# An SSM branch fused into a projection pass: paired output products, paired in-chunk kernels, one scan per part, and a higher scheduling level

## The chip, the cores and the metric

The kernel runs on one NeuronCore of a Trainium2 chip. The metric is the device time of one execution in microseconds (us), the median over several runs. The engines are TensorE (PE, with its weight loads PEld), VectorE (DVE), ScalarE (ACT), GpSimd (POOL) and SyncE (SP), which here issues every DMA of the program.

## The reference

One layer of a hybrid encoder over 2048 prompt tokens and 64 sample tokens, D = 1024, all in float32. `x @ w_in` gives q, k, v and u, 512 columns each. q and k go through a partial rotary and into differential attention (8 heads, two softmax maps each, block-causal mask). u goes through a diagonal SSM and a gated linear unit (GLU). Both halves meet in `@ w_out`, then follow a layer norm, a feed-forward block with 4096 hidden columns, and a second layer norm. The part that matters here is the SSM:

```
32 groups of 16 channels, each with 64 complex states:
  h[l] = lb * h[l-1] + (bb_re + i bb_im) u[l]        prompt from 0, sample from the state h0
  y[l] = Re(C h[l]) + d * u[l]
  z    = gelu(y) @ w_glu + b_glu ; out = z[:512] * sigmoid(z[512:])
```

## The kernel before

**Chunks.** The 2048 prompt steps are cut into 256 chunks of T = 8 steps and the sample into 8; with one column kept for the sample's starting state there are NJ = 265 columns. Within a chunk the SSM is a matrix product with a kernel matrix `km`; between chunks it is a scan over the 265 columns.

**Batches.** The 32 groups are worked in four batches of 8 groups, which lie in four pairs: group 2q on partitions 0 to 63, group 2q+1 on 64 to 127 (64 states each). `ssm_build` makes a batch's matrices: `bb`, `em` (input to state), `gf` (state to output), the kernels `psk` (PE products of `bb` and `gf`, 64 states by 16 channels, one group at a time), which go by way of the DRAM tensor `KP` into `km`, and the turning factors `et` (some 40 POOL instructions). `ssm_run` loads `ug`, makes the states' inputs `psi` on PE, copies them from PSUM into `z` (real part by ACT, imaginary part by DVE), turns `z` into `v` with `et` (5 DVE instructions), scans, turns back, and then makes one output product `psy` a group: two matmul instructions of 128 rows with `km`, then four of 64 rows with `gf` and `v`. GELU follows as Square (ACT), a DVE instruction, Tanh (ACT), a DVE instruction, and a DMA into the DRAM tensor `GY`. Every float32 matmul shows as two instructions in the trace.

**Buffers.** `psy` has two PSUM banks (`PSB`), `psi` and `psk` share two (`IB`), `gy` has two buffers (`GB`), `z`, `vt`, `vx`, `em` and `et` one each. `ep` in the building and `vx` in the run share one slot.

**Order.** A planner orders each engine's instructions ahead of time: among those that are ready by its own simulated time it takes the one of highest priority, which is program order unless a `level(n)` raises it. While the pass for q and k (`proj_qk`, 17 tiles of 128 tokens; PE tile `pm`, transposes `pt`, outputs `s_q`, `s_k`) is written out, ten steps of the SSM generator are written after each of its tiles (`R1`), so that all SSM steps stand in program order among the first four tiles. `level(U8)` around them is 0, so nothing is raised. From the seventh tile `cache_keys` adds its own copies. After the pass follows the attention, at a level above all of this (`HIP`), whose output accumulator `oT` needs a PSUM bank that the SSM holds until its end; and GLU (`za`, `zb`, `gyg`, `whg`) as filling, which needs all of `GY`. On PE a full-size product in the pass is three matmuls (`mm3`).

Of the kernel before, what the change touches and what calls it, by code (L numbers as in the profile page):

```python
# [67 lines left out]
WGB = 2  # L68
PARTS = [1, 0, 0, 0]
A0S = 0  # L70
U8 = 0
VVB = 2
VB = 2
U5, U6 = 2, 0
# [39 lines left out]
def build(nc, tc, io, ctx):  # L114
# [25 lines left out]
    def tt(e, out, a, b, op):  # L140
        e.tensor_tensor(out=out, in0=a, in1=b, op=op)  # L141
# [529 lines left out]
    def ssm_disc(kp, sp):  # L671

        NC_ = G // 2
        k.ss = ss = K()
        a = sp.tile([128, 3, NC_], F32, name="adisc")
        dma(out=a, in_=io["adisc"])
        sh = [128, NC_]
        t = lambda nm: (kp if nm in ("fr", "fi", "rho") else sp).tile(sh, F32, name=nm)
        dt, x, mag, ang = t("dt"), t("xx"), t("mag"), t("ang")
        exp_exact(sp, dt, a[:, 2], sh, "dx")  # L680
        tt(dve, x, a[:, 0], dt, ALU.mult)
        exp_exact(sp, mag, x, sh, "dx")
# [24 lines left out]
        tt(dve, fr, fr, t2, ALU.add)  # L707
        tt(dve, fr, fr, den, ALU.mult)
        tt(dve, fi, li, a[:, 0], ALU.mult)
        tt(dve, t2, nr, a[:, 1], ALU.mult)  # L710
        tt(dve, fi, fi, t2, ALU.subtract)
        tt(dve, fi, fi, den, ALU.mult)
        ss.fr, ss.fi = fr, fi

        ss.rho = rho = t("rho")
        tt(dve, rho, mag, mag, ALU.mult)
        tt(dve, rho, rho, rho, ALU.mult)
        tt(dve, rho, rho, rho, ALU.mult)
        ss.u = kp.tile([128, 2, 8, NC_], F32, name="uu")
        q = sp.tile([128, 2, NC_], F32, name="uq")  # L720
        for n in range(10):
            w = ss.u[:, :, n - 2] if n > 1 else sp.tile([128, 2, NC_], F32, name="uv%d" % (n + 1))
            tt(dve, q, v, v, ALU.mult)
            dve.scalar_tensor_tensor(out=w[:, 1], in0=v[:, 0], scalar=2.0, in1=v[:, 1], op0=ALU.mult, op1=ALU.mult)
            tt(dve, w[:, 0], q[:, 0], q[:, 1], ALU.subtract)
            tt(dve, q, w, w, ALU.mult)
            tt(dve, q[:, 0], q[:, 0], q[:, 1], ALU.add)
            dve.tensor_scalar(out=q[:, 0], in0=q[:, 0], scalar1=-0.5, scalar2=1.5, op0=ALU.mult, op1=ALU.add)
            tt(dve, w, w, b2(q[:, 0]), ALU.mult)
            v = w  # L730
        ss.zz = kp.tile([C, 1, 112], F32, name="zz")
        pool.memset(ss.zz, 0.0)
        dma(out=KP[:, :, 0:112], in_=ss.zz.to_broadcast([C, G, 112]))
        ss.dsb = kp.tile([C, G], F32, name="dsb")
        dma(out=ss.dsb, in_=io["dT"])
        ss.fin = kp.tile([128, 2, 2, 16], F32, name="hfin")

# [8 lines left out]
    def ssm_build(w, bt):  # L746

        ss = k.ss  # L750
        HG = SSM_HG
        HP = HG // 2
# [4 lines left out]
        m.km = w.kp.tile([128, HG, 128], F32, tag="km", name="km", bufs=MB)  # L757
        m.em = w.kp.tile([128, HP, 2, 128], F32, tag="em", name="em", bufs=1)
        m.gf = w.kp.tile([128, 2, HP, 9, C], F32, tag="gf", name="gf", bufs=MB)
        m.et = w.kp.tile([128, 2, HP, NJ], F32, tag="et", name="et", bufs=EB)  # L760
        bc = bp.tile([128, 2, 2, HP, C], F32, tag="bc", name="bc")
        dma(out=bc[:, 0], in_=io["bP"][:, :, qs, :])
# [31 lines left out]
            act.activation(out=m.em[:, :, ri, :], in_=pse, func=AF.Copy)  # L794
        powers(m.gf, bc[:, 1], 9, True)
        yield
        k0 = bp.tile([128, HG, 128], F32, tag="btm", name="k0")[0:C]
        dd = bp.tile([C, HG, C], F32, tag="dd", name="dd")
        for e in range(2):
            psk = pm.tile([C, HP, 128], F32, tag="pi", name="psk", bufs=IB)  # L800
            o = slice(e * 64, e * 64 + 64)
            for q in range(HP):
                for ri in range(2):
                    pe.matmul(psk[:, q, :], lhsT=bb[o, ri, q, :], rhs=m.gf[o, ri, q, 0:8, :].rearrange("p t c -> p (t c)"),
                              start=ri == 0, stop=ri == 1)
            act.activation(out=k0.rearrange("c (q e) n -> c e q n", e=2)[:, e], in_=psk, func=AF.Copy)
        tt(dve, dd, ss.dsb[:, gs].unsqueeze(2).to_broadcast([C, HG, C]), ident[0:C, 0:C].unsqueeze(1).to_broadcast([C, HG, C]), ALU.mult)
        tt(dve, k0[:, :, 0:C], k0[:, :, 0:C], dd, ALU.add)
        dma(out=KP[:, gs, 112:240], in_=k0)
        for n in range(T):  # L810
            dma(out=m.km[n * C:(n + 1) * C, :, :], in_=KP[:, gs, n * C:n * C + 128])

# [4 lines left out]
        for l in range(1, 8):  # L817
# [3 lines left out]
            for ri in range(2):  # L821
                tt(pool, e[:, ri, :, n:2 * n], e[:, ri, :, 0:n], ss.u[:, 0, l, qs].unsqueeze(2).to_broadcast([128, HP, n]), ALU.mult)
                tt(pool, tmp[:, ri], e[:, 1 - ri, :, 0:n], us, ALU.mult)
                tt(pool, e[:, ri, :, n:2 * n], e[:, ri, :, n:2 * n], tmp[:, ri], (ALU.subtract, ALU.add)[ri])
        pool.tensor_copy(out=e[:, :, :, JP:NJ], in_=e[:, :, :, 0:NJ - JP])
        w.mats = m
        yield

    def ssm_run(w, m, bt):
# [7 lines left out]
        for s in range(T):  # L837
            dma(out=ug[(7 - s) * C:(8 - s) * C, :, :], in_=US.rearrange("(g c) s j -> s c g j", c=C)[s, :, gs, :])

        z = bp.tile([128, 2, HP, NJ], F32, tag="z", name="z", bufs=ZB)  # L840
        vt = bp.tile([128, 2, HP, NJ + 1], F32, tag="vt", name="vt")
        v = vt[:, :, :, 1:NJ + 1]
        vx = bp.tile([128, HP, NJ], F32, tag="vx", name="vx")
# [3 lines left out]
        for q in range(HP):  # L847
            for ri in range(2):
                psi = pm.tile([128, 512], F32, tag="pi", name="psi", bufs=IB)
                for e in range(2):  # L850
                    o = slice(e * 64, e * 64 + 64)
                    pe.matmul(psi[o, :NJ], lhsT=m.em[:, q, ri, o], rhs=ug[:, 2 * q + e, :], start=True, stop=True)
                if ri == 0:
                    act.activation(out=z[:, ri, q, :], in_=psi[:, :NJ], func=AF.Copy)
                else:
                    dve.tensor_copy(out=z[:, ri, q, :], in_=psi[:, :NJ])
            if q % 2:
                yield
        dve.tensor_copy(out=z[:, :, :, JP], in_=h0)
# [7 lines left out]
        turn(v, z, (ALU.add, ALU.subtract))  # L867
        yield
        for ri in range(2):
            for q in range(HP):  # L870
                for c0, c1, i in ((0, JP, 0.0), (JP + 1, NJ, h0[:, ri, q:q + 1])):
                    dve.tensor_tensor_scan(out=z[:, ri, q, c0:c1], data0=ss.rho[:, bt * HP + q:bt * HP + q + 1].to_broadcast([128, c1 - c0]),
                                           data1=v[:, ri, q, c0:c1], initial=i, op0=ALU.mult, op1=ALU.add)
        turn(v, z, (ALU.subtract, ALU.add))
        for i, j in enumerate((JP - 1, NJ - 1)):
            pool.tensor_copy(out=ss.fin[:, i, :, qs], in_=v[:, :, :, j])
        yield
        for g in range(HG):
            psy = pm.tile([128, 512], F32, tag="ps", name="psy")
            y = psy[:, :NJ]  # L880
            o = slice(g % 2 * 64, g % 2 * 64 + 64)
            pe.matmul(y, lhsT=m.km[:, g, :], rhs=ug[:, g, :], start=True, stop=False)
            for ri in range(2):
                pe.matmul(y, lhsT=m.gf[o, ri, g // 2, 1:9, :].rearrange("p t c -> p (t c)"), rhs=vt[o, ri, g // 2, 0:NJ], start=False, stop=ri == 1)

            gy = sp.tile([128, NJ], F32, tag="gy", name="gy", bufs=GB)
            act.activation(out=gy, in_=y, func=AF.Square, scale=math.sqrt(0.044715))
            dve.scalar_tensor_tensor(out=gy, in0=gy, scalar=1.0, in1=y, op0=ALU.add, op1=ALU.mult)
            act.activation(out=gy, in_=gy, func=AF.Tanh, scale=GC)
            dve.scalar_tensor_tensor(out=gy, in0=gy, scalar=1.0, in1=y, op0=ALU.add, op1=ALU.mult)  # L890
            gg = bt * HG + g
            dma(out=GY[gg * C:(gg + 1) * C, :, :].rearrange("c t j -> t c j"), in_=gy)
            if g % 4 == 3:
                yield

    def ssm_all(c2):
# [562 lines left out]
```

## Time and profile before

| what | value |
|---|---|
| median of 3 runs | 3173.56 us (3170.77 to 3175.68) |
| the profiled execution | 3174.97 us |
| its span, first to last instruction | 3173.1 us |
| PE busy | 2909.3 us (92%) |
| DVE busy | 1761.8 us (56%) |
| ACT busy | 1504.2 us (47%) |
| POOL busy | 1636.2 us (52%) |

Outside the span lie 1.9 us. Busy shares are averages over stages with different limits; the pass for q and k with the SSM fills roughly 209 to 527 us of the span, the start of the attention 527 to 590 us, and after that attention, GLU and the feed-forward blocks share the engines.

### The profile page before, as it was taken

The numbers are of one execution on the slowest core, as the hardware profiler recorded it, in microseconds if no ns is written. First come the engines' busy times: TensorE is split into PE (matmuls) and PEld (weight loads), VectorE is DVE, ScalarE is ACT, GpSimd is POOL, SyncE is SP. The second block draws the span as 40 slices with busy tenths as digits, with TensorE's granted clock in tenths as the row PEclk, the third lists the DMA queues.
The fourth block names the chain that finished last, engine by engine and source line by source line (L and its number), as shares of the span: only waits on it lengthen the run. The fifth ranks groups of instructions, "written<-read, shape, count | busy, mean of one in ns | idle before, by whom it ended". The sixth has DMA issues, their size and how long they took to land.

```text
span 3173.1 us, 46490 instructions
## 1 busy us (share of the span) xinstructions
PE 2909.3 (92%) x15648; PEld 2423.9 (76%) x15648; DVE 1761.8 (56%) x4631; ACT 1504.2 (47%) x2905; POOL 1636.2 (52%) x1552
## 2 busy tenths in 40 slices
PE   8999998998898999998689999986899998899996
PEld 7976666896687888786589888864777776788885
DVE  7126866677867665567876666654222226322225
ACT  3222223776775766665567766522232322332332
POOL 2236761455654666565546666534445544544443
PEclk9999998798899999998789999998899998899998
DMA  6368875658534444446434333265223322422221
GB/s 189 128 194 212 219 204 166 202 155 276 147 107 131 130 134 119 119 118 213 144 114 129 100 110 107 76 230 179 74 83 94 89 83 80 130 80 77 80 84 56
DMA packets 420195, 425.47 MB, mean 134 GB/s; under 512 B 53458, under 2 KB 313042, under 8 KB 418932
## 3 DMA queue, kind: packets, MB, share of 16 engines
q1 hardware_dynamic: 419956, 422.50, 45.0%
q8 instruction: 123, 2.02, 0.3%
q14 instruction: 116, 0.95, 0.1%
HBM read 328.76 MB, written 93.64 MB: 133 GB/s over the span
## 4 chain that ended last, share of the span: by engine, by line
PE 55%; DVE 12%; DMA 11%; POOL 6%; issue 4%; ACT 3%; SPq 1%; POOLq 0%; DVEq 0%; ACTq 0%
PE pd L136 7%; PE pd L137 7%; PE pd L138 7%; PE pu L136 5%; PE pu L138 5%; PE pu L137 5%; DMA raw<-in_w_up 4%; PE oT L575 4%; PE tps L559 3%; PE sps L512 3%; DMA raw<-in_w_down 2%; POOL dl L133 2%; POOL fwl L133 2%; DVE acc L141 2%; DMA raw<-in_ln_g 2%
## 5 line engine op out<-in xcount | busy, mean ns | idle before, releaser
L133 POOL TENSOR_TENSOR dl<-raw,dh 128x512 fp32r<-128x512 f32 x336 | 432.8, 1301 | 294.5 <-ACT dh L130 286.3
L133 POOL TENSOR_TENSOR fwl<-raw,fwh 128x512 fp32r<-128x512 f32 x256 | 332.3, 1300 | 380.2 <-ACT fwh L130 355.3
L136 PE MATMUL pu<-bxh,fwh 128*128 128x256 f32 (+2 forms) x1472 | 496.3, 339 | 26.0 <-ACT fr L1167 17.0
L515 DVE TENSOR_SCALAR_CACHE_REDUCE s<-sps 128x512 f32<-128x512 f32 (+5 forms) x688 | 402.9, 600 | 210.9 <-PE sps L512 132.3
L141 POOL TENSOR_TENSOR s<-s 128x512 f32<-128x512 f32 (+3 forms) x344 | 382.6, 1139 | 237.4 <-ACT s L543 237.0
L138 PE MATMUL pu<-bxh,fwl 128*128 128x256 f32 (+2 forms) x1472 | 491.4, 337 | 7.0 <-POOL fwl L133 6.1
L137 PE MATMUL pu<-bxl,fwh 128*128 128x256 f32 (+2 forms) x1472 | 490.6, 334 | 0.0
L136 PE MATMUL pd<-dh,hh 128*128 128x512 f32 (+1 forms) x1088 | 426.5, 400 | 18.6 <-DVE acc L141 10.1
L137 PE MATMUL pd<-dl,hh 128*128 128x512 f32 (+1 forms) x1088 | 430.8, 396 | 0.7 <-POOL dl L133 0.7
L141 DVE TENSOR_TENSOR acc<-acc,pd 128x512 f32<-128x512 f32 (+1 forms) x384 | 254.3, 682 | 302.1 <-PE pd L138 300.8
L523 ACT ACTIVATE s<-s,nm 128x1024 f32<-128x1024 f32 (+9 forms) x416 | 365.8, 881 | 116.7 <-DVE nm L520 113.0
L138 PE MATMUL pd<-dh,hl 128*128 128x512 f32 (+1 forms) x1088 | 419.5, 396 | 0.0
L130 ACT ACTIVATE dh<-raw 128x512 fp32r<-128x512 f32 x336 | 209.2, 628 | 353.8 <-PE pd L138 209.1
L130 ACT ACTIVATE fwh<-raw 128x512 fp32r<-128x512 f32 x256 | 160.5, 628 | 378.9 <-DMA raw<-in_w_up 243.0
L136 PEld LDWEIGHTS pu<-bxh,fwh 128*128 128x128 f32 x1472 | 283.7, 193 | 68.9 <-ACT fr L1167 28.5
L132 DVE CAST hh<-fr 128x256 fp32r<-128x256 f32 (+2 forms) x184 | 111.2, 604 | 397.3 <-ACT fr L1168 397.0
L138 PEld LDWEIGHTS pu<-bxh,fwl 128*128 128x128 f32 x1472 | 282.2, 193 | 40.7 <-POOL fwl L133 15.3
L137 PEld LDWEIGHTS pu<-bxl,fwh 128*128 128x128 f32 x1472 | 283.8, 193 | 26.4
L575 PE MATMUL oT<-w,vt 128*128 128x256 f32 (+3 forms) x1296 | 258.2, 301 | 18.2 <-DVE w L133 12.8
L136 PEld LDWEIGHTS pd<-dh,hh 128*128 128x128 f32 (+1 forms) x1088 | 202.0, 186 | 63.1 <-DVE acc L141 12.0
L575 PEld LDWEIGHTS oT<-w,vt 128*128 128x128 f32 (+1 forms) x1296 | 211.3, 202 | 48.1 <-DVE w L133 20.4
L512 PE MATMUL sps<-kst,qst 96*128 96x512 f32 (+2 forms) x544 | 218.6, 419 | 20.9 <-DVE s L515 18.5
(273 smaller groups left out, 5890.0 us busy)
## 6 DMA issues: line engine op xcount, KB each, us to landing
raw<-in_w_up SPq DMA_DIRECT2D x256, 256.0 KB
raw<-in_w_down SPq DMA_DIRECT2D x256, 256.0 KB
kst<-s_k SPq DMA_DIRECT2D x64, 384.0 KB
raw<-in_w_out SPq DMA_DIRECT2D x80, 256.0 KB
xr<-in_xT SPq DMA_DIRECT2D x64, 256.0 KB
vt<-s_v SPq DMA_DIRECT2D x32, 512.0 KB
qst<-s_q SPq DMA_DIRECT2D x64, 192.0 KB
raw<-in_ln_g SPq DMA_DIRECT2D x36, 256.0 KB
```

What stands on the lines that cost most here:

```text
L130: act.activation(out=dst_hi, in_=src, func=AF.Copy)
L132: hi_eng.tensor_copy(out=dst_hi, in_=src)
L133: (lo_eng or dve).tensor_tensor(out=dst_lo, in0=src, in1=dst_hi.bitcast(F32), op=ALU.subtract)
L136: pe.matmul(ps, lhsT=lh, rhs=rh, start=start, stop=False)
L137: pe.matmul(ps, lhsT=lh, rhs=rl, start=False, stop=False)
L138: pe.matmul(ps, lhsT=ll, rhs=rh, start=False, stop=stop)
L141: e.tensor_tensor(out=out, in0=a, in1=b, op=op)
L512: pe.matmul(ps[:nr, :e - c0], lhsT=qst[m][0:96, q], rhs=self.keys(m, 96, c0, e), start=True, stop=True)
L515: dve.tensor_scalar(out=s[:nr, o:o + c1 - c0], in0=ps[:nr, :c1 - c0], scalar1=1.0, scalar2=None, op0=ALU.mult, op1=ALU.max, accum_out=self ...
L523: act.activation(out=x, in_=x, func=AF.Exp, bias=nm, accum_out=self.ls[:nr, m, p:p + 1])
L559: pe.transpose(out=ps[:kr, i * nr:i * nr + nr], in_=self.s[t, 0, k_ * 128 // SC][:nr, o:o + kr], identity=ident[:nr, :nr])
L575: pe.matmul(self.oT[:, t * nr:(t + n) * nr], lhsT=vt[k_ // 8][:kr, k_ % 8, :], rhs=w[:kr, e, i * nr:(i + n) * nr], start=(k_ == 0 and e == ...
```

## The change

Five things are changed, all in the SSM. (1) `U8 = 1`: the SSM's steps have a raised level and stand ahead of the pass in the planner's choice. (2) The output products are made for the two groups of a pair in turn: both `km` products, then for the real and the imaginary part one `gf` product of each group; the GELU instructions of the two are interleaved. (3) The kernels within a chunk are made by pairs: `bz` holds `bb` of both groups beside zeros, so that one product of 128 rows and 32 columns replaces two of 64 rows and 16 columns; `dsb`, `id2`, `dd`, `k0` follow that layout, and the write into `KP` becomes two DMAs. (4) One scan of 4 x 266 columns for each of real and imaginary part replaces 16 scans a batch: a factor table `rh`, zero at the first column and at the sample's start, cuts it. (5) The copies of `psi` into `z` all go to ACT.

```diff
-U8 = 0
+U8 = 1
...
-        ss.dsb = kp.tile([C, G], F32, name="dsb")
+        ss.dsb = kp.tile([2 * C, G // 2], F32, name="dsb")
+        ss.id2 = kp.tile([2 * C, C], F32, name="id2")
+        tt(dve, ss.id2, ident[0:2 * C, 0:C], ident[0:2 * C, C:2 * C], ALU.add)
...
+        m.rh = w.kp.tile([128, HP, NJ + 1], F32, tag="rh", name="rh", bufs=EB)
...
+        bz = bp.tile([128, 2, HP, 2, C], F32, tag="bz", name="bz")
+        pool.memset(bz, 0.0)
         for e in range(2):
-            psk = pm.tile([C, HP, 128], F32, tag="pi", name="psk", bufs=IB)
             o = slice(e * 64, e * 64 + 64)
-            for q in range(HP):
-                for ri in range(2):
-                    pe.matmul(psk[:, q, :], lhsT=bb[o, ri, q, :], rhs=m.gf[o, ri, q, 0:8, :]...
-            act.activation(out=k0.rearrange("c (q e) n -> c e q n", e=2)[:, e], in_=psk, func=AF.Copy)
+            pool.tensor_copy(out=bz[o, :, :, e, :], in_=bb[o])
+        psk = pm.tile([2 * C, HP, 128], F32, tag="pi", name="psk", bufs=IB)
+        for q in range(HP):
+            for ri in range(2):
+                pe.matmul(psk[:, q, :], lhsT=bz[:, ri, q]..., rhs=m.gf[:, ri, q, 0:8, :]...
+        act.activation(out=k0, in_=psk, func=AF.Copy)
...
-        dma(out=KP[:, gs, 112:240], in_=k0)
+        for e in range(2):
+            dma(out=KP.rearrange("c (q e) n -> e c q n", e=2)[e, :, qs, 112:240], in_=k0[e * C:e * C + C])
...
+        pool.tensor_copy(out=m.rh, in_=ss.rho[:, qs].unsqueeze(2).to_broadcast([128, HP, NJ + 1]))
+        pool.memset(m.rh[:, :, 0:JP + 2:JP + 1], 0.0)
...
-                if ri == 0:
-                    act.activation(out=z[:, ri, q, :], in_=psi[:, :NJ], func=AF.Copy)
-                else:
-                    dve.tensor_copy(out=z[:, ri, q, :], in_=psi[:, :NJ])
+                act.activation(out=z[:, ri, q, :], in_=psi[:, :NJ], func=AF.Copy)
...
-            for q in range(HP):
-                for c0, c1, i in ((0, JP, 0.0), (JP + 1, NJ, h0[:, ri, q:q + 1])):
-                    dve.tensor_tensor_scan(out=z[:, ri, q, c0:c1], data0=ss.rho[...].to_broadcast([128, c1 - c0]),
-                                           data1=v[:, ri, q, c0:c1], initial=i, op0=ALU.mult, op1=ALU.add)
+            dve.tensor_tensor_scan(out=zt[:, ri]..., data0=m.rh..., data1=vt[:, ri]...,
+                                   initial=0.0, op0=ALU.mult, op1=ALU.add)
...
-        for g in range(HG):
-            (one psy: km product, two gf products, GELU, DMA)
+        for q in range(HP):
+            ys = [pm.tile([128, 512], F32, tag="ps", name="psy")[:, :NJ] for e in range(2)]
+            for e, y in enumerate(ys):
+                pe.matmul(y, lhsT=m.km[:, 2 * q + e, :], rhs=ug[:, 2 * q + e, :], start=True, stop=False)
             for ri in range(2):
+                for e, y in enumerate(ys):
+                    o = slice(e * 64, e * 64 + 64)
+                    pe.matmul(y, lhsT=m.gf[o, ri, q, 1:9, :]..., rhs=vt[o, ri, q, 0:NJ], start=False, stop=ri == 1)
+            (Square and first DVE instruction of both, then Tanh, second DVE instruction and DMA of both)
```

## Rows read from the trace of the kernel before

**Rows 1.** Busy time by stretch (us of each engine, instructions; TensorE clock, DMA share, GB/s).

```profile
209.00:527.00 318.00, 296.02 (x1397) 212.30 (x1398) 225.69 (x347) 90.88 (x189) 191.54 (x295) 0.97 0.77 204
...
527.00:590.00 63.00, 47.88 (x164) 34.87 (x164) 35.46 (x141) 38.30 (x105) 15.44 (x20) 0.55 0.81 251
590.00:720.00 130.00, 129.76 (x1076) 128.70 (x1076) 95.78 (x374) 101.72 (x262) 72.03 (x93) 0.99 0.51 154
```

**Rows 2.** PE in order of time, batch 2 (start us, us, what; idle before).

```profile
392.11 0.72 PE L884 MATMUL psy<-vt,gf 64*128 64x265 f32 x4
392.76 0.67 PE L852 MATMUL psi<-ug,em 128*64 128x265 f32 x4
...
398.55 0.71 PE L882 MATMUL psy<-ug,km 128*128 128x265 f32 x2
399.19 1.16 PE L884 MATMUL psy<-vt,gf 64*128 64x265 f32 x4
400.28 0.71 PE L882 MATMUL psy<-ug,km 128*128 128x265 f32 x2
```

**Rows 3.** PE in order of time, the kernels of batch 2.

```profile
298.23 3.24 PE L804 MATMUL psk<-gf,bb 64*16 64x128 f32 x32 [1.76 <-POOL gf L141]
301.40 0.50 PE L136 MATMUL pm<-wh,xh 128*128 128x512 f32 x1
```

**Rows 4.** Instructions by line (count; busy us, mean ns of one; idle before).

```profile
L872 DVE TENSOR_TENSOR_SCAN z<-rho,vt 128x256 f32<-128x256 f32 x32 | 22.6, 706 | 0.0
L872 DVE TENSOR_TENSOR_SCAN z<-rho,h,vt 128x8 f32<-128x8 f32 x32 | 6.8, 214 | 0.0
L854 ACT ACTIVATE z<-psi 128x265 f32<-128x265 f32 x16 | 6.2, 390 | 33.0 <-DVE vx L141 21.9 <-PE psi L852 11.1
L806 ACT ACTIVATE k<-psk 16x512 f32<-16x512 f32 x8 | 4.6, 578 | 8.8 <-PE psk L804 5.1 <-POOL cvv L133 2.8 <-issue 0.8
L132 POOL CAST ckh<-ckr 128x512 fp32r<-128x512 f32 x8 | 5.3, 668 | 6.8 <-DMA ckr<-in_ckT 6.3 <-issue 0.5
```

**Rows 5.** DVE in order of time: turns of the first and the last batch.

```profile
281.75 3.35 DVE L141 TENSOR_TENSOR vt<-z,et 128x2120 f32<-128x2120 f32 x1 [1.85 <-POOL et L141]
305.68 1.25 DVE L141 TENSOR_TENSOR vt<-vt,vx 128x1060 f32<-128x1060 f32 x1
492.99 2.37 DVE L141 TENSOR_TENSOR vt<-z,et 128x2120 f32<-128x2120 f32 x1 [0.87 <-PE psy L884]
500.58 1.25 DVE L141 TENSOR_TENSOR vt<-vt,vx 128x1060 f32<-128x1060 f32 x1
516.16 1.26 DVE L141 TENSOR_TENSOR vt<-vt,vx 128x1060 f32<-128x1060 f32 x1
```

**Rows 6.** ACT in order of time: batch 1's building, and a copy into z.

```profile
245.97 0.63 ACT L130 ACTIVATE xh<-xr 128x512 fp32r<-128x512 f32 x1 [9.28 <-DMA xr<-in_xT]
247.98 1.08 ACT L794 ACTIVATE em<-pse 128x512 f32<-128x512 f32 x2
390.45 0.39 ACT L854 ACTIVATE z<-psi 128x265 f32<-128x265 f32 x1 [11.63 <-DVE vx L141]
```

**Rows 7.** The output products' tile: one cause of its idle time (us, times).

```profile
  DMA s_gy<-gy: 17.7, 8
```

**Rows 8.** PE in order of time: last matmul of the pass, first oT.

```profile
523.39 0.39 PE L138 MATMUL pm<-wh,xl 128*128 128x512 f32 x1
560.63 1.11 PE L575 MATMUL oT<-w,vt 128*128 128x256 f32 x4 [0.35 <-DVE gy L890]
```

**Rows 9.** SP's issues in order of time (start us, us, transfer, how many).

```profile
421.02 3.27 SPq L125 DMA_DIRECT2D ug<-s_u  x7
523.80 0.59 SPq L125 DMA_DIRECT2D s_gy<-gy  x1
539.97 1.35 SPq L125 DMA_DIRECT2D s_gy<-gy  x2
```

**Rows 10.** Waits, 209 to 527 us (us in total, times, longest).

```profile
ACT xh L130 <- DMA xr<-in_xT: 54.2, 14, 9.3
```

More of the change, by code (lines that the diff above doesn't have):

```diff
@@ L796, in ssm_build @@
         yield
-        k0 = bp.tile([128, HG, 128], F32, tag="btm", name="k0")[0:C]
-        dd = bp.tile([C, HG, C], F32, tag="dd", name="dd")
+        k0 = bp.tile([128, HG, 128], F32, tag="btm", name="k0")[0:2 * C, 0:HP]
+        dd = bp.tile([2 * C, HP, C], F32, tag="dd", name="dd")
+        bz = bp.tile([128, 2, HP, 2, C], F32, tag="bz", name="bz")
+        pool.memset(bz, 0.0)
         for e in range(2):
-            psk = pm.tile([C, HP, 128], F32, tag="pi", name="psk", bufs=IB)
             o = slice(e * 64, e * 64 + 64)
-            for q in range(HP):
-                for ri in range(2):
-                    pe.matmul(psk[:, q, :], lhsT=bb[o, ri, q, :], rhs=m.gf[o, ri, q, 0:8, :].rearrange("p t c -> p (t c)"),
-                              start=ri == 0, stop=ri == 1)
-            act.activation(out=k0.rearrange("c (q e) n -> c e q n", e=2)[:, e], in_=psk, func=AF.Copy)
-        tt(dve, dd, ss.dsb[:, gs].unsqueeze(2).to_broadcast([C, HG, C]), ident[0:C, 0:C].unsqueeze(1).to_broadcast([C, HG, C]), ALU.mult)
+            pool.tensor_copy(out=bz[o, :, :, e, :], in_=bb[o])
+        psk = pm.tile([2 * C, HP, 128], F32, tag="pi", name="psk", bufs=IB)
+        for q in range(HP):
+            for ri in range(2):
+                pe.matmul(psk[:, q, :], lhsT=bz[:, ri, q].rearrange("p e c -> p (e c)"), rhs=m.gf[:, ri, q, 0:8, :].rearrange("p t c -> p (t c)"),
+                          start=ri == 0, stop=ri == 1)
+        act.activation(out=k0, in_=psk, func=AF.Copy)
+        tt(dve, dd, ss.dsb[:, qs].unsqueeze(2).to_broadcast([2 * C, HP, C]), ss.id2.unsqueeze(1).to_broadcast([2 * C, HP, C]), ALU.mult)
         tt(dve, k0[:, :, 0:C], k0[:, :, 0:C], dd, ALU.add)
-        dma(out=KP[:, gs, 112:240], in_=k0)
+        for e in range(2):
+            dma(out=KP.rearrange("c (q e) n -> e c q n", e=2)[e, :, qs, 112:240], in_=k0[e * C:e * C + C])
         for n in range(T):
@@ L838, in ssm_run @@
             dma(out=ug[(7 - s) * C:(8 - s) * C, :, :], in_=US.rearrange("(g c) s j -> s c g j", c=C)[s, :, gs, :])
-        z = bp.tile([128, 2, HP, NJ], F32, tag="z", name="z", bufs=ZB)
+        zt = bp.tile([128, 2, HP, NJ + 1], F32, tag="z", name="z", bufs=ZB)
+        z = zt[:, :, :, 1:NJ + 1]
         vt = bp.tile([128, 2, HP, NJ + 1], F32, tag="vt", name="vt")
@@ L869, in ssm_run @@
         for ri in range(2):
-            for q in range(HP):
-                for c0, c1, i in ((0, JP, 0.0), (JP + 1, NJ, h0[:, ri, q:q + 1])):
-                    dve.tensor_tensor_scan(out=z[:, ri, q, c0:c1], data0=ss.rho[:, bt * HP + q:bt * HP + q + 1].to_broadcast([128, c1 - c0]),
-                                           data1=v[:, ri, q, c0:c1], initial=i, op0=ALU.mult, op1=ALU.add)
+            dve.tensor_tensor_scan(out=zt[:, ri].rearrange("p q j -> p (q j)"), data0=m.rh.rearrange("p q j -> p (q j)"),
+                                   data1=vt[:, ri].rearrange("p q j -> p (q j)"), initial=0.0, op0=ALU.mult, op1=ALU.add)
         turn(v, z, (ALU.subtract, ALU.add))
@@ L877, in ssm_run @@
         yield
-        for g in range(HG):
[L879 to L882, printed above, removed]
-            for ri in range(2):
[L884 to L893, printed above, removed]
+        for q in range(HP):
+            ys = [pm.tile([128, 512], F32, tag="ps", name="psy")[:, :NJ] for e in range(2)]
+            for e, y in enumerate(ys):
+                pe.matmul(y, lhsT=m.km[:, 2 * q + e, :], rhs=ug[:, 2 * q + e, :], start=True, stop=False)
+            for ri in range(2):
+                for e, y in enumerate(ys):
+                    o = slice(e * 64, e * 64 + 64)
+                    pe.matmul(y, lhsT=m.gf[o, ri, q, 1:9, :].rearrange("p t c -> p (t c)"), rhs=vt[o, ri, q, 0:NJ], start=False, stop=ri == 1)
+            gs_ = [sp.tile([128, NJ], F32, tag="gy", name="gy", bufs=GB) for e in range(2)]
+            for y, gy in zip(ys, gs_):
+                act.activation(out=gy, in_=y, func=AF.Square, scale=math.sqrt(0.044715))
+                dve.scalar_tensor_tensor(out=gy, in0=gy, scalar=1.0, in1=y, op0=ALU.add, op1=ALU.mult)
+            for e, (y, gy) in enumerate(zip(ys, gs_)):
+                act.activation(out=gy, in_=gy, func=AF.Tanh, scale=GC)
+                dve.scalar_tensor_tensor(out=gy, in0=gy, scalar=1.0, in1=y, op0=ALU.add, op1=ALU.mult)
+                gg = bt * HG + 2 * q + e
+                dma(out=GY[gg * C:(gg + 1) * C, :, :].rearrange("c t j -> t c j"), in_=gy)
+            if q % 2:
                 yield
@@ L1435 @@
         bP=bP, cP=cP,
-        dT=f["ssm_d"][0].T, h0=np.stack([pair(f["state_ssm_re"][0, 0]), pair(f["state_ssm_im"][0, 0])], 1),
+        dT=f["ssm_d"][0].reshape(16, 2, C).transpose(1, 2, 0).reshape(2 * C, 16), h0=np.stack([pair(f["state_ssm_re"][0, 0]), pair(f["state_ssm_im"][0, 0])], 1),
         w_glu=f["w_glu"][0], bglu=f["b_glu"][0].reshape(8, 128).T, w_out=f["w_out"][0],
```

## The prediction

> **What bounds the kernel now.** I read the busy time by stretch first, then each engine's instructions in order of time around the SSM, then the waits. The stretch in which the pass for q and k runs with the SSM, 209 to 527 us, has TensorE busy for 296.02 of 318 us at a granted clock of 0.97 of full speed (2.4 GHz) [rows 1]. No other engine comes near: DVE 225.69, POOL 191.54. So PE work that is taken out shortens the pass almost one for one, as long as nothing else in it becomes late. The next stretch, 527 to 590 us, is the weak one: PE is busy for 47.88 of 63 us at a mean clock of 0.55, mostly the lower of its two levels, 1.2 GHz. Worked out as 47.88 x 0.55, that is 26 us of work at full clock, so some 37 us are lost there. After it PE is full again: 129.76 of 130 us at 0.99 [rows 1].
>
> Why is that stretch weak? The pass issues its last matmul at 523.39, but the attention's first `oT` starts at 560.63, right after the SSM's last `gy` instruction [rows 8]: `oT` needs a bank that the SSM holds. GLU waits for the whole of `GY` as well. So the second bound is the end of the SSM, a chain of latencies over four batches. In order of time on DVE, the first batch begins to turn at 281.75 and the last at 492.99: (492.99 - 281.75) / 3 = 70.4 us a batch. From there the last batch needs 516.16 + 1.26 - 492.99 = 24.4 us for turn, scan and turn [rows 5], and the first batch's first turn was 281.75 to 306.93, 25.2 us, where the last one's was 492.99 to 501.83, 8.8 us. That leaves 70.4 - 24.4 - 16.4 = about 30 us a batch for the output products and their GELU, before `vt` is free for the next batch. What slows the products is not PE: ACT stood 17.7 us in 8 waits until a `GY` write had let a `gy` buffer go [rows 7]. And when the pass ends with the SSM still running, the attention's loads come between: one `GY` write issues at 523.80 and the next two at 539.97 [rows 9].
>
> The time therefore hangs on two things: how much earlier the pass ends, and how much earlier the SSM ends.
>
> **PE's share.** A group's products take 1.73 us today (398.55 to 400.28: two `km` instructions, 399.19 - 398.55 = 0.64, and four `gf`, 1.09 [rows 2]). What two groups in turn cost is already in the trace: in each batch the first pair, whose `km` products were done early, waits for `vt` and then runs so. At 392.11 four `gf` instructions of two groups (64 rows each, different halves of the array) take until 392.76, 0.65 us, where four of one group take 1.09 [rows 2]. A pair after the change: two runs of four such instructions in a row, bounded above by 2 x 0.65 = 1.30, less the second change of shape between them (four instructions of a shape cost 1.09 when serial, two cost 0.64, so an instruction is 0.225 and the entry and exit of a shape 0.19 together): 1.30 - 0.19 = 1.11; and four `km` instructions in one go, 0.64 + 2 x 0.225 = 1.09. Sum 2.2 against 2 x 1.73 = 3.46, a gain of 1.26 us a pair. Four of the sixteen pairs are paired already, so 12 x 1.26 = 15 us. If the planner puts other products between and the halves don't overlap, only the changes of shape are saved, 2 x 0.19 x 12 = 5 us. I take 15, since the trace shows the overlap for this very shape; the range keeps 5.
>
> The kernels within a chunk: 32 instructions took 3.24 us, to 301.40 with what follows [rows 3], so about 0.1 us each. Sixteen replace them. Full-height products of 128 columns are not in that row; at the same length each batch saves 1.6, in all 6 us; were they twice as long, nothing. I take 6, as the streamed columns, 128, stay the same. Together 21 us, bounds 5 and 21.
>
> **DVE, ACT, POOL, SP.** Scans: 32 of 256 columns at 706 ns and 32 of 8 at 214 ns, 29.4 us in all [rows 4]. The slope is (706 - 214) / 248 = 1.98 ns a column, so one of 4 x 266 = 1064 columns is 214 + 1056 x 1.98 = 2.3 us, and eight are 18.5: 11 us less, all on the chain, 2.7 a batch. If a factor read from a table instead of one value a row cost more per column, up to half more, eight would be 27 and the gain 2; I take 11, as an instruction of the same class is the nearest row. The imaginary copies of `psi` leave DVE for ACT: 16 x 390 ns = 6.2 us more there, less four `k` copies at 578 ns, 2.3 [rows 4]; ACT is busy for 90.88 of 318 us [rows 1], and this hides. Its danger is position: a copy into `z` already held ACT for 11.63 us until the last batch had let `z` go [rows 6], with the pass's own copies behind it. That wait keeps its place, it only ends earlier if the chain does. POOL gets one `rh` copy of 1064 columns a batch (at 668 ns for 512 [rows 4], 1.4 us), two copies and one clearing for `bz` (under 1 us by the same row) and a tiny clearing: some 2.5 us a batch, 10 in all, beside 126 us of idle. `rh` is needed only after the turn of 8.8 us, `bz` only for kernels that are used a batch later; without that cover the cost would be the same 10 us. SP issues four more writes at 3.27 / 7 = 0.47 us [rows 9], 2 us, hidden by the same distance to `km`.
>
> **The raised level.** All SSM steps already stand among the pass's first four tiles in program order, so the level alters only the start: there the pass's first tiles, and loads written before, go ahead today. Two prices are in the trace. ACT stood 9.28 us for an x load at 245.97, and the SSM's `em` copy came behind it at 247.98 [rows 6]; with `em` in front the chain starts up to 9 us earlier. And the first turn of batch 1 took 25.2 us instead of 8.8, with the pass's work in between; bounds 0 and 16.4, I take half, 8, because part of the gap is the building of batch 2, which keeps its level. Below nothing: its transfers now stand before the pass's x loads on SP (the slower rival, below).
>
> **The output products' tail.** With two `gy` buffers taken and let go as a pair, the bound by the `GY` writes stays, so for the 30 us a batch I count no gain; interleaved GELU could save some, the joint release could cost some.
>
> At one place a rule of the Trainium skill speaks against the change. TensorEngine Tiling, section PSUM Bottleneck, says that tiling quickens TensorE but not the emptying of PSUM, which can become the limit, and advises ScalarE and VectorE together for it; the change pairs the products and gives all `psi` copies to one of the two. By that rule the pairs bring the chain nothing, which is what the 17.7 us of waiting for `gy` [rows 7] already leave me counting; the sum is the same without the sentence, and the rule's own outcome is the second rival.
>
> **Sum.** The pass ends 21 us earlier, near 502 instead of 523. The chain gains 9 + 8 + 11 = 28 us: the last turn ends near 489 instead of 517. Its products need the 30 us of the earlier batches where the last batch, disturbed by the attention's loads, needed 560.6 - 517.4 = 43. So `oT` can start near 520 instead of 560.63: 40 us earlier. What follows is shifted as a whole, since PE is full from 590 on. Profiled execution: 3174.97 - 40 = 3135 us. Its own time is 1.4 above the median of the runs shown (3173.56), which I ignore.
>
> **Rivals.**
> - *Only PE work arrives (0.27).* The SSM still ends late enough for the attention's loads to come between its `GY` writes, as at 523.80 to 539.97 [rows 9]; the stretch keeps its shape and moves by the pass's 21 us: 3154. For it: pass and SSM shorten by about the same. If the halves don't overlap either (the change then not doing what it says), 3165.
> - *Emptying and `GY` writes set the pace (0.10).* Pairs hold both banks and both `gy` buffers until both are through; the products of a batch get slower by what the scan and the start save, so that of the chain's 28 us some 18 go. Gain 10: 3165. For it the waits for `GY` [rows 7]; against it that both groups' GELU steps alternate between two engines.
> - *The SSM ends well before the pass (0.11).* Then nothing of the weak stretch's 37 us [rows 1] is lost, beside the 21: 3117. For it the full raise of the first turn (16 instead of 8) and faster products.
> - *The raised level starves the pass (0.11).* ACT waited for x loads 14 times, 54.2 us in all [rows 10], and each batch puts eight `ug` and eight `km` transfers on SP, seven of them 3.27 us [rows 9], so 3.7 us for eight. If each of the 14 waits gets one such run in front and PE stands for it, that is 52 us against 21 + 10 gained: 3175 + 21 = 3196. It decides from about 9 of 14 on. Against it: only the first tiles fall in the raised part, and PE was busy in 93% of the stretch in spite of those waits.
> - *No measurable change (0.05):* both ends move by less than the order of later work is disturbed.
>
> **Numbers.** The forecast has 0.36. About 0.2% (6 us) is what a measurement of this kernel can tell from no change. Faster takes the forecast, the first and third rival and most of the second: 0.36 + 0.27 + 0.11 + 0.08 = 0.82. Slower 0.11, same 0.07. The range runs from 3106, the third rival with half of the pass's own idle PE time gone too (318 - 296.02 = 22 us [rows 1], so 11), up to 3168, which takes in the second rival and the pairs without overlap; it leaves out the slower rival, no change, and the far ends of the others, about 0.2.
>
> **What would show it.** `gf` instructions of a pair starting together, near 2.2 us a pair; eight scans of about 2.3 us; 64 `psk` instructions; `em` of batch 1 before 245; the last matmul of the pass near 502, the last turn near 489, the first `oT` near 520; in the stretch after the pass a clock well over 0.55. The prediction is wrong if `oT` still starts over 30 us after the pass ends, if the batch period stays at 70 us, or if the waits for x loads grow past 100 us.

## The result: slower, and the profile after

The changed kernel takes 3255.93 us (median of 4 runs, 3253.94 to 3258.55) against 3173.8: a ratio of 1.026 [1.0242, 1.0278], where 3135 was forecast. The profiled execution is 3253.94 us with a span of 3252.2, 79.1 more than before's 3173.1.

Stretches of the changed kernel, with the columns of [rows 1]:

```profile
209.00:527.00 318.00, 288.95 (x1352) 212.07 (x1352) 213.68 (x265) 95.10 (x207) 183.50 (x283) 0.94 0.64 160
527.00:590.00 63.00, 35.93 (x135) 28.54 (x134) 32.39 (x149) 32.28 (x94) 15.49 (x20) 0.54 0.86 252
590.00:720.00 130.00, 102.94 (x410) 84.57 (x411) 99.67 (x399) 84.22 (x196) 58.14 (x65) 0.57 0.69 208
...
527.00:760.00 233.00, 173.37 (x777) 144.03 (x777) 164.44 (x642) 150.33 (x354) 99.37 (x113) 0.62 0.70 210
760.00:1980.00 1220.00, 1136.60 (x6600) 970.97 (x6600) 857.39 (x2466) 828.50 (x1586) 721.58 (x631) 0.96 0.45 135
1980.00:3252.00 1272.00, 1149.53 (x5658) 938.62 (x5656) 425.42 (x877) 372.65 (x652) 605.65 (x489) 0.96 0.33 100
```

The same for the kernel before, the stretch that rows 1 do not hold:

```profile
590.00:760.00 170.00, 159.43 (x1220) 153.16 (x1219) 127.71 (x473) 126.23 (x306) 90.31 (x109) 0.95 0.62 195
```

The pass ends about where it did (its last matmul at 525.5 us, for 523.8). What is new is that the weak stretch lasts until after 720 us: from 590 to 720 there are 410 matmuls where there were 1076 [rows 1], at 0.57 of full speed, close to the lower level of 1.2 GHz. Busy time times clock gives the work done at full clock. From 527 to 760 that was 47.88 x 0.55 + 159.43 x 0.95 = 177.8 us before and is 173.37 x 0.62 = 107.5 now: some 70 us are missing. They are made up later, where the engine does 1136.60 x 0.96 / 1220 = 0.89 and 1149.53 x 0.96 / 1272 = 0.87 us of such work per us. 70.3 / 0.88 = 80 us, about the 79.1 us between the two spans.

Why is there too little to do? SP's issues in order of time, changed kernel:

```profile
549.03 1.28 SPq L125 DMA_DIRECT2D s_gy<-gy  x2
...
560.59 0.36 SPq L125 DMA_DIRECT2D cvr<-in_cv  x1
...
717.58 0.34 SPq L125 DMA_DIRECT2D s_kc<-ckl  x1
...
722.21 1.75 SPq L125 DMA_DIRECT2D wrg<-in_w_glu  x2
```

And before, the first load of the cache:

```profile
212.86 1.05 SPq L125 DMA_DIRECT2D cvr<-in_cv  x1
```

`cache_keys`, which the diff does not touch, starts at 560.59 in place of 212.86, behind the last writes of `gy` into `GY` (549.03). Its copies then run beside the attention, and the last store is issued at 717.58. GLU's weights (`wrg`) follow at 722.21, and its first product stands at 729.5 where it was at 579.0 (PE in the tile view of `za`, changed kernel, then before):

```profile
L136 PE MATMUL za<-gh,whg x128: 276/281/369, 729.5 to 878.6; 128*128 128x256 f32 x112, 128*128 128x320 f32 x16
```

```profile
L136 PE MATMUL za<-gh,whg x128: 276/281/415, 579.0 to 721.0; 128*128 128x256 f32 x112, 128*128 128x320 f32 x16
```

So from about 533 to 729 PE has little but the attention, which cannot fill it.

The theory is one of room. A pool is the run of bytes that a group of tiles shares in each partition, and pools used at different times may lie on the same bytes. In the program as it is built, the SSM's tiles end at byte 98,084 of each partition and the cache copies' pool begins at 101,280: 3,196 bytes are free. The change adds `rh` (4 x 266 x 4 = 4,256 bytes), `bz` (1,024) and 32 in `z`, and takes 256 from `dd`: 5,056 more, 1,860 too many. What reaches over are the two `gy` buffers, the last tiles of the SSM. The first cache tile then lies on room that the SSM uses to its last `gy`, and its load has to stand behind the last `GY` write. GLU's staging pool lies in part on the cache copies' room and waits in turn. The rivals: the raised level moved the cache copies back in the planner's order, or the parts themselves cost the time.

### The profile page after: what moved, and what is told of

Its sections match the earlier page's. It is cut to its first block, busy times and chain, and to the rows that moved or that the text cites. A ratio compares the mean times of both kernels' runs of the same rounds, so it can differ in the third digit from the quotient of the medians.

```text
span 3252.2 us, 46434 instructions
## 1 busy us (share of the span) xinstructions
PE 2945.5 (91%) x15584; PEld 2440.5 (75%) x15584; DVE 1740.8 (54%) x4560; ACT 1507.9 (46%) x2917; POOL 1657.7 (51%) x1572
## 4 chain that ended last, share of the span: by engine, by line
PE 55%; DMA 15%; DVE 11%; POOL 7%; issue 6%; ACT 4%; SPq 2%; POOLq 0%; DVEq 0%; ACTq 0%
PE pd L136 6%; PE pd L137 6%; PE pd L138 6%; PE pu L136 6%; PE pu L138 6%; PE pu L137 6%; DMA raw<-in_w_up 4%; PE oT L575 3%; POOL fwl L133 3%; PE tps L559 2%; PE sps L512 2%; DMA raw<-in_w_down 2%; POOL dl L133 2%; DVE s L515 2%; DVE acc L141 2%
## 5 line engine op out<-in xcount | busy, mean ns | idle before, releaser
L575 PE MATMUL oT<-w,vt 128*128 128x256 f32 (+3 forms) x1296 | 268.8, 311 | 21.9 <-DVE w L133 10.4
L512 PE MATMUL sps<-kst,qst 96*128 96x512 f32 (+2 forms) x544 | 228.2, 442 | 40.5 <-DVE s L515 38.5
L136 PEld LDWEIGHTS pd<-dh,hh 128*128 128x128 f32 (+1 forms) x1088 | 201.2, 185 | 57.8 <-DVE acc L141 9.9
```

The costliest lines, as they stand in the source:

```text
L136: pe.matmul(ps, lhsT=lh, rhs=rh, start=start, stop=False)
L512: pe.matmul(ps[:nr, :e - c0], lhsT=qst[m][0:96, q], rhs=self.keys(m, 96, c0, e), start=True, stop=True)
L575: pe.matmul(self.oT[:, t * nr:(t + n) * nr], lhsT=vt[k_ // 8][:kr, k_ % 8, :], rhs=w[:kr, e, i * nr:(i + n) * nr], start=(k_ == 0 and e == ...
```

## Experiments

The kernel before was timed again beside each set of runs (medians of 3166.36 to 3167.5 us), and each ratio goes by the one beside it.

**Room alone, on the kernel before.** An unused tile beside the SSM's others; nothing else. The first has the 5,056 bytes of the change, the second 2,880, which fit.

```
+        m.pad = w.kp.tile([128, 1264], F32, tag="pad", ...)   # second kernel: 720
+        pool.memset(m.pad[:, 0:8], 0.0)
```

> The kernel before, with one unused table of 1264 columns (5056 bytes a partition, what the change adds to the SSM's tiles) in the SSM's pool, cleared in 8 columns a batch; nothing of the change itself. Theory 'room': the SSM's tiles then reach into the place of the cache copies' tiles, the cache copies wait for the SSM's end, and GLU's staging tiles wait for them: about 3255 us (+80), first cache load after 540 us, first GLU product near 720 us. Rival 'level' (steps ahead of the pass starve it) and rival 'pairs and scan' (the new instructions are slower): 3174 us, within 6.

> The kernel before, with an unused table of 2880 bytes a partition in the same place, which still leaves the cache copies' tiles free. Theory 'room': 3174 us, within 6, first cache load near 213 us. The rivals expect 3174 too; a slowdown of tens of us here would mean that a tile in this pool costs by itself, whatever it covers.

Measured: 3249.45 us, 1.0272 [1.0236, 1.0308], and 3167.76 us, 1.0004 [0.9993, 1.0016]. The stretches and the cache load of the first:

```profile
527.00:590.00 63.00, 34.23 (x123) 26.91 (x124) 32.88 (x152) 30.64 (x90) 18.03 (x24) 0.53 0.82 238
590.00:720.00 130.00, 106.90 (x425) 87.24 (x425) 103.05 (x403) 91.29 (x207) 64.72 (x71) 0.58 0.72 221
...
544.21 0.53 SPq L125 DMA_DIRECT2D cvr<-in_cv  x1
...
703.62 0.92 SPq L125 DMA_DIRECT2D wrg<-in_w_glu  x2
```

A tile in which eight columns are written and none read makes the whole loss, with the same long weak stretch. The size decides, not the tile: the smaller one costs nothing that shows.

**The change with room, and with the level undone.** The cache copies' tiles are cut from 6 to 4 KB (third kernel), the level is put back (fourth), both (fifth).

```
-                vv = op.tile([...], F32R, tag="ck" + t_, name="cvv")
+                vv = op.tile([...], F32R, tag="ckh", name="cvv")
-                l = op.tile([128, 512], F32R, tag="ckl", name="ckl")
+                l = raw.bitcast(F32R)
-U8 = 1
+U8 = 0
```

> The changed kernel, with the cache copies' tiles cut from 6 KB to 4 KB a partition (both value halves share one slot, the low key part is written over the raw tile), so that they lie clear of the SSM's tiles; all five parts of the change stay. Theory 'room': the cache copies start near 213 us, GLU's first product comes near 540 to 570 us, and the time falls below the kernel before, 3125 to 3165 us. Rival 'level' and rival 'pairs and scan': still about 3255 us.

> The changed kernel with the SSM's level put back to 0; pairs, kernels by pairs, one scan and their tiles stay. Theory 'room': still 3240 to 3265 us, GLU's first product still near 720 us. Rival 'level': back to 3174 us or below. Rival 'pairs and scan': 3255 us.

> The changed kernel with the smaller tiles for the cache copies and the SSM's level back at 0: pairs, kernels by pairs and one scan without the overlap and without the raise. With the overlap gone the changed kernel ran at the time of the one before (3168 against 3166), its pass ending 23 us later, with 82 us of ACT's waits for x loads instead of 54. Theory 'the raise starves the pass and eats what the parts save': 3130 to 3155 us, the waits for x loads back under 60 us. Rival 'the parts save nothing because the planner's order and the GY writes set the pace': 3160 to 3172, whatever the level.

Measured: with room 3167.84 us, 1.0000 [0.9986, 1.0014]; with the level undone and no room 3246.6, 1.0256 [1.0235, 1.0278]; with both 3145.32, 0.9926 [0.9906, 0.9946]. With room, the tile view of `cvr` (its first and last start in the middle) reads:

```profile
L125 SPq DMA_DIRECT2D cvr<-in_cv x8: 351/498/1279, 214.4 to 356.5; - x8
```

The room is the whole of the loss, and the level has no part in it. But the gain that was expected with room (3125 to 3165 us) did not come: the parts bring nothing with the level and 0.7% without. The latter is the best version found, so once there is room the level costs what the rest brings.

**The level alone, and the change with the old 64 scans kept** (`rh` left out, so that it fits).

> The kernel before with the SSM's level raised to 1 and nothing else. Its tiles stay clear of the cache copies' tiles. Theory 'the raise starves the pass': 3176 to 3196 us against 3166, the pass ending 10 us or more later, the waits for x loads near 80 us. Rival 'the raise is nothing, because SSM steps stand among the first four tiles anyway': 3166, within 6.

> The changed kernel without part 4: the 64 scans as before and no factor table, everything else changed, the cache copies' tiles at full size. The SSM's tiles grow by only 800 bytes a partition and stay clear. Theory 'room': the 80 us are gone, 3150 to 3180 us, the cache loads from near 213 us on. Rival 'the paired products or the raise cost the 80 us': 3240 or more.

Measured: 3173.8 us, 1.0015 [0.9994, 1.0036], and 3173.1, 1.0017 [1.0002, 1.0032]. By itself the raised level is worth nothing that shows, though its runs spread widely (3152.73 to 3187.38 us) and its trace is of the fastest of them. Pairs and kernels by pairs with that level, and with room, gain nothing either.

**The cache copies ahead in the planner's order,** room still short:

```
+                    with level(3):
                         next(ck, None)
-            run(ck)
+            run(urgent(ck, 3))
```

> The changed kernel as it is, with the overlap, and the steps of the cache copies raised to level 3, above the attention. They still can't start before the SSM's end, but then go ahead of the attention. Theory 'GLU waits for the last cache copy': the copies finish within 40 to 80 us instead of 160, GLU's first product comes right after the last one, near 600 to 640 us instead of 729, and the time is 3180 to 3215 us. Rival 'GLU waits for something else': GLU's first product stays near 729 and the time near 3250.

Measured: 3223.68 us, 1.0171 [1.0149, 1.0193]. The copies still start at 561.2, since they wait for room, but end sooner, and GLU with them, though less than was expected (a first product at 600 to 640 and 3180 to 3215 us):

```profile
686.12 0.41 SPq L125 DMA_DIRECT2D s_kc<-ckl  x1
...
690.65 0.83 SPq L125 DMA_DIRECT2D wrg<-in_w_glu  x2
...
L136 PE MATMUL za<-gh,whg x128: 276/281/416, 697.4 to 847.4; 128*128 128x256 f32 x112, 128*128 128x320 f32 x16
```

GLU's first product comes 32.1 us earlier (697.4 for 729.5), and the span of the profiled execution falls by 27.9 us, from 3252.2 to 3224.3. That ties the loss to the end of the cache copies and the start of GLU. It gives no price by the us: from the kernel before to the changed one GLU starts 150.5 us later for 79.1 us of span, and with the level undone it starts at 735.8, later still, with a span of 3243.2.

**Where the 0.7% comes from:** the kernel before with the smaller cache tiles alone, and the best version without its paired products.

> The kernel before with nothing changed but the two smaller tile sets of the cache copies (4 KB in place of 6 KB), which it has room for anyway: the control for the version with room and without the raised level (3145.3). If that version's 21 us came from the SSM's parts, this one stays at the kernel before, 3166 plus or minus 8. If they came from the smaller set of tiles or from the order that the planner writes around it, this one shows them too, near 3145. The SSM's end (first oT) should stay near 560 either way.

> The version with room and without the raised level, and without the products in pairs: group by group as before, with the kernels by pairs and the one scan kept. If the pairs make that version's gain (3145.3 against 3166.7), this one goes back to about 3166. If the gain comes from the scan and the kernels it stays near 3145. If the gain is the planner's order, it can come out anywhere between 3145 and 3175, with no part to put it down to.

Measured: 3173.61 us, 1.002 [1.0007, 1.0032], and 3169.9, 1.0001 [0.9989, 1.0012]. So the smaller tiles do not bring it, and it goes when the pairs go. The first of these kernels is the best version's control: the two differ by the parts of the change alone. Against it the best version gains 28.3 us by the medians, where it gains 21.4 beside the kernel before. PE at the end of the pass and at the first `oT`, and the work up to 760 us and to 2040, in the control:

```profile
542.85 0.39 PE L138 MATMUL pm<-wh,xl 128*128 128x512 f32 x1
...
579.68 0.58 PE L575 MATMUL oT<-w,vt 128*128 128x256 f32 x1 [0.58 <-ACT w L130]
...
0.00:760.00 760.00, 682.25 (x3879) 558.11 (x3880) 449.86 (x1208) 300.37 (x694) 338.32 (x472) 0.93 0.64 186
760.00:2040.00 1280.00, 1210.27 (x6634) 1023.31 (x6634) 880.32 (x2530) 856.84 (x1607) 767.51 (x644) 0.95 0.45 133
```

The same in the best version, and the rest of its span:

```profile
523.27 0.39 PE L138 MATMUL pm<-wh,xl 128*128 128x512 f32 x1
...
557.21 1.18 PE L575 MATMUL oT<-w,vt 128*128 128x256 f32 x4
...
0.00:760.00 760.00, 692.49 (x3923) 574.43 (x3924) 459.18 (x1224) 321.60 (x743) 363.58 (x501) 0.93 0.66 191
760.00:2040.00 1280.00, 1210.94 (x6677) 1025.62 (x6676) 877.76 (x2482) 859.62 (x1605) 782.44 (x655) 0.97 0.44 131
2040.00:3140.00 1100.00, 983.83 (x4988) 811.38 (x4986) 395.92 (x855) 323.47 (x570) 510.84 (x418) 0.95 0.33 102
```

The pass ends 19.6 us earlier and `oT` starts 22.5 us earlier. The kernels by pairs save 64 PE instructions, so at 760 us the best version is 3923 + 64 - 3879 = 108 of them ahead, and gains 43 more to 2040. Most of its lead over the control arises where the parts of the change lie. Beside the kernel before it looks otherwise:

```profile
760.00:2040.00 1280.00, 1197.01 (x6578) 1014.65 (x6579) 889.03 (x2532) 856.18 (x1604) 765.06 (x642) 0.95 0.44 128
2040.00:3173.00 1133.00, 1013.03 (x5090) 834.65 (x5089) 404.13 (x833) 331.34 (x582) 526.35 (x430) 0.95 0.33 101
```

At 760 us that kernel is level with the best version (3982 against 3923 + 64), and it falls 99 behind only then, in a stretch that contains none of the change. The smaller tiles alone end the pass 19.5 us later (543.2 for 523.8) and yet cost only 0.2%. How that kernel makes this up is not settled; an order of later work that the planner wrote differently fits, but it is argued, not shown.

**Four `gy` buffers:** in the change with the old scans and level, and in the kernel before (`GB = 4`).

> The changed kernel with the old 16 scans a batch (so that it fits), without the raised level, and with four gy buffers in place of two. If the GY writes hold the products back through the two buffers, ACT's waits for gy (26 us in 12 waits in the version with the old scans) fall below 5 us, the period of a batch falls by several us and the SSM ends 10 us or more earlier: 3130 to 3155. If the products are held back by what stands ahead of them on PE in the planner's order, the waits go and the SSM's end stays: 3160 to 3175.

> The kernel before with four gy buffers in place of two and nothing else changed. The 17.7 us of waits for gy go. If those waits were on the SSM's path, its end (first oT at 560.6) comes about 10 us earlier and the time falls to about 3155. If the order of the planner sets the end, the time stays within 0.2% of 3166.

Measured: 3152.63 us, 0.995 [0.993, 0.9969], and 3154.65, 0.9953 [0.9936, 0.9971]. The waits for `gy` are gone (0.9 us are left in the second kernel), and the times are those expected of "the `GY` writes hold the products", but not by way of the start of the attention. The kernel before with four buffers, DVE and then PE in order of time:

```profile
550.91 0.43 DVE L890 SCALAR_TENSOR_TENSOR gy<-gy,psy 128x265 f32<-128x265 f32 x1 [0.49 <-ACT gy L889]
564.19 0.69 DVE L133 TENSOR_TENSOR tpl<-pt,tph 128x512 fp32r<-128x512 f32 x1 [12.84 <-DMA s_q<-tpl]
...
567.27 0.87 PE L559 MATMUL tps<-ident,s 128*128 128x128 f32 x3 [17.74 <-DVE hb L931]
...
569.10 1.18 PE L575 MATMUL oT<-w,vt 128*128 128x256 f32 x4
```

The last `gy` is done at 551.3, some 9 us earlier than in the kernel before, and the first `oT` comes 8.5 us later than at 560.63 [rows 8]. In between DVE waits 12.84 us to split the pass's last q and k, because a store of an earlier tile has not landed. SP's view shows that store's issue taking 4.54 us; what made it slow is not settled.

**A third tile for that split,** with the smaller cache tiles, and the same with three `gy` buffers.

```
-            h = op.tile([128, 4, 128], F32R, tag="tph", name="tph")
+            h = op.tile([128, 4, 128], F32R, tag="tph", name="tph", bufs=3)   # tpl likewise
```

> The kernel before with the smaller tiles of the cache copies (its control is 3173.6) and three tiles in place of two for each half of the split q and k. If the stores of the pass's last tiles hold the first oT, the split no longer waits for them, and oT follows the last product or the last split closely, some 5 to 15 us earlier than the control's 579.7, near 565. If oT needs the SSM's end, it stays where the last gy instruction is, near 560 to 565, whatever the split does. On the time: if the start of the attention bounds the rest, as the prediction took it, every us of it comes off, 3160 to 3168; if not, it stays within 0.3% of 3173 in either direction.

> The same with three gy buffers too, so that the SSM's products wait less for the GY writes and both of the things that could hold the first oT are relieved. If the prediction's view of the stretch after the pass holds, with the store in place of the SSM as the second holder, oT comes near 545 to 550 and the time falls by 10 us or more against the control, to 3163 or less. If oT comes earlier and the time does not follow, the start of the attention is not what the end hangs on. If oT stays near 560 or later, a third thing holds it: the attention's own loads, which stand in SP's order among these stores.

Measured: 3166.57 us, 0.9996 [0.9981, 1.0011], and 3169.99, 1.0003 [0.9991, 1.0016]. PE of the first:

```profile
566.39 0.77 PE L514 MATMUL sps<-kst,qst 99*128 99x128 f32 x2 [8.71 <-DMA qst<-s_qm]
566.96 0.84 PE L559 MATMUL tps<-ident,s 128*128 128x128 f32 x3
569.12 0.52 PE L575 MATMUL oT<-w,vt 128*128 128x256 f32 x1
```

`oT` moves from the control's 579.7 to 569.1, or 573.7 with three `gy` buffers, and the time by 7 and 4 us of 3173.6, less than the control's own runs spread (12.4 us). The 3166.57 lies in both of the ranges that were expected, so this pair does not decide. The split still waits for a store (4.61 us on DVE), and a third holder shows: the attention's own q loads. Over the versions with room, `oT` lies between 555.1 (old scans, 3173.1 us) and 579.7 (smaller cache tiles, 3173.61), and 3153 us go with `oT` at 569.7. Across them the time does not follow it. Among the six kernels with the smaller cache tiles it does at the ends: 557.2 goes with the fastest, 3145.32, and 579.7 with the slowest, 3173.61, while 569.0 to 575.8 all give 3167 to 3170.

## Why the prediction was wrong

**The step that failed is "DVE, ACT, POOL, SP".** It costed `rh` and `bz` by their instructions and by how late each is needed, and asked what each step waits for; it did not ask where the tiles lie and whose room they take. All 79 us come from that: the padded kernel, with the room taken and none of the change, loses as much (1.0272 for 1.026). No rival contained it: "the raised level starves the pass" had the right sign (3196), but the waits for x loads fell, from 54.2 [rows 10] to 33.9 us, and undoing the level leaves 1.0256. With the room given, the rest of the sum was still short: 3167.84 us where 3135 was forecast, with the terms below.

**"PE's share" had its parts right at the full clock, and its consequence came in some versions only.** A pair, the kernels of a batch, and the stretch of the pass in the padded kernel, which has none of the change and whose cache copies have left the pass too:

```profile
525.95 1.06 PE L887 MATMUL psy<-ug,km 128*128 128x265 f32 x4
526.94 1.16 PE L891 MATMUL psy<-vt,gf 64*128 64x265 f32 x8
528.03 0.87 PE L349 MATMUL pt<-ident,qk 128*128 128x128 f32 x6
...
293.29 1.72 PE L811 MATMUL psk<-gf,bz 128*32 128x128 f32 x14
...
209.00:527.00 318.00, 301.70 (x1424) 215.55 (x1424) 212.51 (x338) 94.37 (x199) 162.00 (x267) 0.98 0.65 167
```

The pair takes 528.03 - 525.95 = 2.08 us (2.2 predicted), and a full-height kernel product 1.72 / 14 = 0.12, little longer than the half-height one's 0.10 [rows 3]. These kernels ran at the full clock; most of those of the other three batches stood at a granted clock of 0.50 to 0.63. Over the whole SSM the kernels took 12.15 us of PE for 15.79, and the products 44.84 for 57.28: 3.6 and 12.4 us where 6 and 15 were counted, with the clock's part in them not taken out.

The pass ended at 525.5 and not at 502. In the padded kernel it ended at 526.0, with 301.70 x 0.98 = 296 us of full-clock work; the changed kernel had 288.95 x 0.94 = 272. So 24 us of work went and the pass kept its length: something else paced it there, and the sentence that PE work "shortens the pass almost one for one" was read from a share and not from a wait. With the cache copies in the pass it came in part: with the old scans the pass ended at 515.6 where it was 523.8 before (521.1 with the level alone), and with the smaller cache tiles at 523.7 in the best version where its control has 543.2, 19.6 of the 21 us, but at 541.7 with the level. What paces it is not settled; `ACT`'s waits for x loads do not sort the versions (33.9 us in the changed kernel, 57.8 in the padded one, 74.6 in the best).

**The chain's terms.** By line, the changed kernel from 209 to 527 us:

```profile
L878 DVE TENSOR_TENSOR_SCAN z<-rh,vt 128x1064 f32<-128x1064 f32 x8 | 21.1, 2648 | 0.0
L807 POOL COPY bz<-bb 64x128 f32<-64x128 f32 x8 | 8.3, 1038 | 0.4
L834 POOL COPY rh<-rho 128x1064 f32<-128x1064 f32 x4 | 7.7, 1913 | 16.4 <-DVE z L878 16.4
```

Eight scans take 21.1 us (18.5 predicted), so they save 8.3, not 11; POOL's additions are 17.6 us with the clearings, not 10, still under cover. Of the raised level's 9 + 8, the 9 did not come: `em` of batch 1 starts at 248.59, no earlier than before's 247.98 [rows 6]. The 8 seem to (from the first turn's start at 282.0 to the first scan at 298.59 it is 16.6 us, for 25.2), but they are not the level's: without it, and without room too, it is 12.5 us, and on the kernel before the level leaves 24.9. The padded kernel, without level or change, has 18.5, so part of it too is the cache copies leaving the pass. The period of a batch fell from 70.4 to 65.2 us (first turns at 282.0 and 477.6), but the padded kernel, which has no part of the change, has 62.7: that gain is the cache copies leaving the pass. With room the period is 73.5, or 69.1 with the level undone.

**"The output products' tail" and its rival.** With room, the waits for `GY` grew as the rival feared, from 17.7 in 8 waits [rows 7] to 31.9 us in 16 in the best version (18.0 in 9 without its pairs). The Trainium skill (TensorEngine Tiling (Array Packing), section PSUM Bottleneck) says that tiling does not speed up what empties PSUM. The trace agrees so far as the pairs made ACT wait longer, but it waited for the DRAM writes of `gy` and not for the emptying itself, which no run here shows as the limit.

**"Sum" failed twice.** `oT` was said to need a bank that the SSM holds, because its last wait was for `gy` [rows 8]. That wait was 0.35 us, so other things it needs had come only just before. In the changed kernel the SSM's last `gy` instruction is over at 532.7, and `oT` starts at 561.68. DVE, and then PE, in order of time:

```profile
532.23 0.43 DVE L899 SCALAR_TENSOR_TENSOR gy<-gy,psy 128x265 f32<-128x265 f32 x1
...
556.03 0.69 DVE L133 TENSOR_TENSOR tpl<-pt,tph 128x512 fp32r<-128x512 f32 x1 [4.63 <-DMA s_q<-tpl]
559.00 0.69 DVE L133 TENSOR_TENSOR tpl<-pt,tph 128x512 fp32r<-128x512 f32 x1 [2.28 <-DMA s_k<-tpl]
...
561.68 1.17 PE L575 MATMUL oT<-w,vt 128*128 128x256 f32 x4
```

The last split of q and k is over at 559.7, 2.0 us before `oT`. In thirteen of the sixteen kernels run, the first `oT` starts 1.6 to 4.0 us after the last of these splits, most of which waited for the stores of earlier tiles; in the other three (the kernel before, the smaller pad, the old scans) it starts within 0.1 us of the last `gy`. So the SSM's bank can be the last thing, but a second one lies close behind it: in the kernel before the last split was over at 556.88, so the SSM's end alone would have moved `oT` by some 2 us (an estimate from these rows). Of the prediction's own signs of being wrong this one came: `oT` starts 36 us after the pass ends.

And "what follows is shifted as a whole" does not hold across versions: 25 us of `oT` between the old scans and the smaller cache tiles left no trace in the time. A later start of GLU, whose matmuls fill the attention's gaps, did cost, 79.1 us of span for 150.5.

## What to carry over

A new tile has two prices, its instructions and its room. Before costing the first, add its bytes to the pool's end and see which pool starts there; if it crosses, everything that is placed on that room waits for the new owner's last use, with nothing in the change's own lines to show it. A releaser with a wait of a few tenths of a us names only the last of several ends: moving it gains no more than the distance to the next. And a version is to be compared with a control that has everything but the change. Beside the kernel before, the best version's pass has the same length; beside its control it is 19.6 us shorter.

## What the runs showed of the hardware

In the changed kernel the four scans of 1064 columns in the last two batches took 2.35 to 2.36 us each, with POOL idle beside them. Of the four that ran beside work on POOL one took 3.40, but one only 2.46. POOL's own instructions became longer too. DVE and then POOL in order of time, first batch and second:

```profile
298.59 5.81 DVE L878 TENSOR_TENSOR_SCAN z<-rh,vt 128x1064 f32<-128x1064 f32 x2
...
297.49 1.36 POOL L141 TENSOR_TENSOR bb<-bb,bt 128x64 f32<-128x64 f32 x1
298.81 3.36 POOL L133 TENSOR_TENSOR xl<-xr,xh 128x512 fp32r<-128x512 f32 x1
302.14 2.38 POOL L141 TENSOR_TENSOR bb<-bb,bt 128x64 f32<-128x64 f32 x1
...
367.06 0.64 POOL L141 TENSOR_TENSOR bb<-bb,bt 128x64 f32<-128x64 f32 x2
```

The same product of 64 columns takes 0.32 us in the second batch, between two scans, 1.36 beside a turn on DVE and 2.38 beside the scans. The two scans of the first batch took 5.81 us for two times 2.36: both engines were slower together.
